# Output product of a gated FFN: where its combined weights lie, which queue carries its side traffic, and how its last visits and its norm are cut

## The chip, the core and the metric

The kernel runs on one core of a Trainium2 chip. A core has TensorE (PE, with its weight loads shown as PEld), VectorE (DVE), ScalarE (ACT), GpSimd (POOL), a queue engine that issues transfers (SP), and sixteen DMA engines that carry out the transfers of all queues. Each engine works through its own list in order; engines wait for each other by semaphores. The metric is the time of one execution on the device in microseconds (us), as the median of several runs.

## What is computed

Two decoder layers on one sequence of 1024 rows and 1024 columns, all in fp32. Layer 0 mixes with differential attention, layer 1 with forgetting attention; after either comes a gated FFN, and after each a LayerNorm of the scaled input plus the result:

```python
D_MODEL, SEQ, DEPTH, D_FF = 1024, 1024, 2, 2816

def conv_ffn(x, w_in, conv_w, conv_b, w_out):
    gate, up = jnp.split(x @ w_in, 2, axis=-1)
    gate = lax.conv_general_dilated(gate, conv_w[:, None, :], ...) + conv_b
    return (jax.nn.silu(gate) * up) @ w_out

for i in range(DEPTH):
    y = diff_attention(h, ...) if i == 0 else forgetting_attention(h, ...)
    h = layer_norm(DEEPNORM_ALPHA * h + y, ln1_g[i], ln1_b[i])
    f = conv_ffn(h, ffn_w_in[i], ffn_conv_w[i], ffn_conv_b[i], ffn_w_out[i])
    h = layer_norm(DEEPNORM_ALPHA * h + f, ln2_g[i], ln2_b[i])
```

## The kernel before

Every fp32 operand is split in a high and a low half (`split`, L83: ScalarE makes the high half at L86, VectorE the low at L88), and a product is three matmuls, high by high, high by low, low by high (`mm3`, L97 to L99). One matmul of 128 rows by 512 columns starts 0.227 us after the last.

**Up product.** `up_steps` makes the FFN's inner values tile by tile, f = 0 to 21, each from seven block products. `take` copies or adds a finished PSUM bank into SBUF (L958 a copy on ScalarE, L960 an addition on VectorE). `gated` does the convolution, the silu and the gating, and stores the tile to DRAM as `ad[f]` (L999). In the last one, f = 21, stands a block of its own (`tile_critical`, L994 to L996) that loads ScalarE's other activation table: ScalarE enters it by a branch.

**Output product.** `down_steps` is a block scheme of seven products m = 1 to 7 over H = 11 k-tiles. With a11, a12, a21, a22 the blocks of the inner values (tiles `ha`, loaded from `ad` by `load_a`) and b11 to b22 those of the weights (`load_b`, from `wd`, into tiles of the pools `pt`, three buffers, and `wst`, two, there named `wb`), it runs four passes over k: m = 1 and 5, then 6 and 3, then 7 and 2, then 4. A pass visits k = 0 to 8 singly and the last two together; the last pass, m = 4, visits 0 to 7 singly and the last `G4` = 3 together. A step is one m and one k: four banks j by three matmuls, 2.72 us. Two combinations of weights are used in more than one pass: T1 = b12 - b11 is made for m = 5 and read again for m = 6, T2 = b22 - T1 is made for m = 6 and read again for m = 4. Before the change both go to DRAM and back, for all eleven k: `sides` stores them (L1078 T1, named `ta`; L1082 T2, `tb`) and `load_b` reloads them into one half of a tile (L1055, L1064) beside a half of `wd`. All combinations are VectorE's, L1071. `make` allots the operand tiles (a ring of six for the left side: `q`, `of` and `p` tiles) and calls `split`.

**Residual, drain and norm.** `load_acc` fetches the eight 128 x 1024 tiles of the scaled residual (`acc` <- `hs`, 512 KB each) into q tiles and one p tile, at step 4 + tt of the product, on SP's queue (L1168). `drain` (L1138, VectorE) adds a finished bank to them. With the last drain of a tile the `Norm` of that tile begins: mean (L1326), squares on ScalarE (L1329, `junk`), root (L1335 to L1343), and `apply`. In `apply` columns from n on are done by VectorE (L1358, L1361), columns below n by ScalarE (L1356) and GpSimd (L1357, L1360), and L1363 stores. For rows tiles 4 to 7 of the last layer n is `PF` = 256.

**What sets the order.** `Ffn.run` walks the steps of the up product and then those of the output product; before step i it calls what is noted for that step (loads, at fixed leads), makes operands until AHEAD = 6 steps ahead, and emits the products. A scheduler then puts the instructions of each engine in one order by their readiness, so that what is emitted late may stand early where an engine is free. GpSimd issues no transfer in this kernel; SP issues all.

## Time and profile before

| | |
|---|---|
| median of 3 runs | 2527.68 us (2524.8 to 2528.6) |
| the profiled execution | 2527.6 us, its span 2525.8 us |
| PE busy | 2460.4 us, 97% of the span |
| DVE busy | 1963.8 us, 78% |
| ACT busy | 1344.6 us, 53% |
| POOL busy | 128.1 us, 5% |
| transfers | 261.67 MB, mean 104 GB/s |

The profile is of one execution. The table above says which engine is the busiest on average; it doesn't say where the time is lost. For that one reads a table of stages (busy time of each engine in stretches of 50 us), then what PE waited for in the stretches where its busy time is short, then the timeline of the engine that it waited for. In a table of stages a row has the stretch, its length, the busy us (and instructions) of PE, PEld, DVE, ACT and POOL, the granted clock as a share of 2.4 GHz, the busy share of the DMA engines and GB/s. In the rows below, `x<-y` means that an instruction writes x from y, a bracket at the end gives the idle time of the engine just before the instruction and what ended it, and a wait reads "engine tile line <- what released it: us in total, times, longest".

In layer 1 the up product ends and the output product begins near 2297 us; it ends with PE at 2512.86. In layer 0 the same runs from about 1028 us on.

### The profile page before, as it was taken

Reading aid. Unit: us, or ns where it says so; the run is one execution under the profiler, and the core shown is the slowest. Engines: PE = TensorE matmul, PEld = TensorE weight load, DVE = VectorE, ACT = ScalarE, POOL = GpSimd, SP = SyncE. Lnnn points to the kernel's source line nnn. Section 1 sums busy time; section 2 is a strip of 40 time slices with the busy share of each in tenths; the row PEclk is TensorE's granted clock in tenths of the full one; section 3 lists DMA queues with packets and bytes.
Section 4 is the critical chain, followed back from the end, with each engine's and each line's share of the span. In section 5 each row is a group of like instructions: output and inputs, shape, how many; then the busy total and the mean of one; then the engine's idle time right before and its main releaser. Section 6 shows DMA issues by size and latency. Waiting matters only on the chain. (4 is left out here: it accounts for less than half of the span.)

```text
span 2525.8 us, 33612 instructions
## 1 busy us (share of the span) xinstructions
PE 2460.4 (97%) x12075; PEld 2021.9 (80%) x12075; DVE 1963.8 (78%) x3770; ACT 1344.6 (53%) x2517; POOL 128.1 (5%) x308
## 2 busy tenths in 40 slices
PE   7999999999999999999999999999999999999997
PEld 5878788787888888788778888888878888888786
DVE  5777777889867667796858888788888667677878
ACT  5666666746544444444546666566465444444444
POOL 0100000001000000000100000000010000000001
PEclk9999999999999999999999999999999999999999
DMA  3111111422322223864411111114222222327744
GB/s 128 34 59 42 43 42 52 167 92 84 109 75 76 100 76 103 315 208 155 158 54 51 51 51 51 46 57 159 91 84 86 98 75 76 100 96 271 246 142 141
DMA packets 94087, 261.67 MB, mean 104 GB/s; under 512 B 11728, under 2 KB 13136, under 8 KB 93920
## 3 DMA queue, kind: packets, MB, share of 16 engines
q1 hardware_dynamic: 93920, 259.53, 30.4%
q8 instruction: 95, 1.56, 0.3%
q14 instruction: 72, 0.59, 0.1%
HBM read 196.44 MB, written 58.85 MB: 101 GB/s over the span
## 5 line engine op out<-in xcount | busy, mean ns | idle before, releaser
L97 PE MATMUL m<-xh,wh 128*128 128x512 f32 x768 | 323.8, 422 | 6.3 <-ACT xh L86 6.2
L99 PE MATMUL m<-xh,wl 128*128 128x512 f32 x768 | 304.9, 397 | 0.0
L98 PE MATMUL m<-xl,wh 128*128 128x512 f32 x768 | 303.9, 396 | 0.2 <-DVE xl L88 0.2
L97 PE MATMUL m<-xh,wo 128*128 128x512 f32 x656 | 255.4, 389 | 2.5 <-ACT pt L958 2.5
L99 PE MATMUL m<-xh,wo 128*128 128x512 f32 x656 | 255.5, 389 | 0.1
L98 PE MATMUL m<-xl,wo 128*128 128x512 f32 x656 | 255.2, 389 | 0.0
L86 ACT ACTIVATE wo<-wg 128x512 fp32r<-128x512 f32 x168 | 106.3, 633 | 226.6 <-PE m L99 218.1
L86 ACT ACTIVATE pt<-m 128x512 fp32r<-128x512 f32 (+1 forms) x240 | 130.0, 553 | 119.7 <-PE m L1225 99.7
L97 PE MATMUL m<-q,wo 128*128 128x512 f32 x472 | 184.1, 390 | 0.0
L98 PE MATMUL m<-q,wo 128*128 128x512 f32 x472 | 183.8, 389 | 0.0
L99 PE MATMUL m<-q,wo 128*128 128x512 f32 x472 | 183.6, 389 | 0.0
L97 PEld LDWEIGHTS m<-xh,wh 128*128 128x128 f32 x768 | 146.7, 191 | 31.0 <-ACT xh L86 6.2
L99 PEld LDWEIGHTS m<-xh,wl 128*128 128x128 f32 x768 | 145.6, 190 | 31.3
L98 PEld LDWEIGHTS m<-xl,wh 128*128 128x128 f32 x768 | 146.7, 191 | 24.9 <-issue 0.8
L86 ACT ACTIVATE wo<-t 128x512 fp32r<-128x512 f32 x132 | 82.8, 627 | 146.6 <-PE m L99 133.3
L88 DVE TENSOR_TENSOR pt<-m,pt 128x512 fp32r<-128x512 f32 (+1 forms) x240 | 149.5, 632 | 9.8 <-ACT pt L86 7.9
L88 DVE TENSOR_TENSOR wo<-wg,wo 128x512 fp32r<-128x512 f32 x168 | 115.3, 687 | 40.2 <-ACT wo L86 39.4
L97 PEld LDWEIGHTS m<-xh,wo 128*128 128x128 f32 x656 | 123.1, 188 | 29.0 <-ACT pt L958 3.3
L99 PEld LDWEIGHTS m<-xh,wo 128*128 128x128 f32 x656 | 123.1, 188 | 26.4 <-DVE wo L88 0.9
L98 PEld LDWEIGHTS m<-xl,wo 128*128 128x128 f32 x656 | 123.1, 188 | 25.5
L410 PE MATMUL s<-q,q 128*128 128x512 f32 (+3 forms) x384 | 135.5, 353 | 3.7 <-ACT q L253 2.5
L403 POOL CAST qz<-q 64x128 fp32r<-64x128 f32 x256 | 88.8, 351 | 952.2 <-PE s L412 670.0
(316 smaller groups left out, 6318.0 us busy)
## 6 DMA issues: line engine op xcount, KB each, us to landing
wst<-in_w SPq DMA_DIRECT2D x48, 512.0 KB, 3.4
t<-in_wi SPq DMA_DIRECT2D x44, 512.0 KB, 4.5
ad<-t SPq DMA_DIRECT2D x44, 512.0 KB, 3.6
ha<-ad SPq DMA_DIRECT2D x88, 256.0 KB, 5.4
wg<-in_wi SPq DMA_DIRECT2D x42, 512.0 KB, 3.3
pt<-in_wd SPq DMA_DIRECT2D x34, 512.0 KB, 3.5
wb<-in_wd SPq DMA_DIRECT2D x42, 256.0 KB, 3.0
wst<-in_wo SPq DMA_DIRECT2D x16, 512.0 KB, 3.5
```

Of the source, the lines that this page charges most:

```text
L86: nc.scalar.activation(hi, src, AF.Copy, scale=1.0 if scale is None else scale)
L88: nc.vector.tensor_tensor(lo, src, hi.bitcast(F32), op=ALU.subtract)
L97: mm(out, wh, xh, start=start, stop=False)
L98: mm(out, wh, xl, start=False, stop=False)
L99: mm(out, wl, xh, start=False, stop=stop)
L403: nc.gpsimd.tensor_copy(qz[r:r + 64, :], q[r:r + 64, qt * P:qt * P + P])
L410: nc.tensor.matmul(sb[:, ks], q[:, qt * P:qt * P + P], kd[:, ks], start=True, stop=False)
```

## The change

Six things are changed. `KH` = 5: T1 and T2 go through DRAM for k = 0 to 4 only, and their stores are issued by GpSimd; for k = 5 to 10 both are kept in halves of three `t` tiles (`hold`), T2 in the place of T1, and only the half of `wd` is loaded. The difference for m = 3 takes turns in the halves of one held `t` tile in place of a new tile each time. The residual is loaded in halves, on GpSimd's queue: the half that is drained first at step 8 + tt, the other at 24 + tt or 40 + tt. While the up product runs, `Ffn.run` makes one operand of the output product ahead before the last step but one and a second before the last, where it made up to six before. The last group of pass 4 is of five k-tiles, `G4` = 5, in both layers. In the last layer's norm of tiles 4 to 7 all columns are VectorE's (`PF` = 0), from `acc` into a `pt` tile and back, and the last tile's final step is two halves with a store each.

```diff
-PF = (256,256,256,256)
+KH = 5
+PF = (0, 0, 0, 0)
-M7, G4 = 15, 3
+M7, G4 = 15, 5
...
+        held = {}
+        def hold(k):
+            if k not in held:
+                t = self.tmp()
+                held[k], held[k + 1] = t[:, lo], t[:, hi]
+            return held[k]
...
             elif n == 1:
-                nc.sync.dma_start(t[:, lo], self.t1[k])
+                if k < KH:
+                    nc.sync.dma_start(t[:, lo], self.t1[k])
                 nc.sync.dma_start(t[:, hi], w[H + k][:, hi])
-                b["t", k], b[22, k] = t[:, lo], t[:, hi]
+                b["t", k], b[22, k] = t[:, lo] if k < KH else hold(k), t[:, hi]
...
             if m == 5:
-                y = sub(b[12, k], b[12, k], b[11, k])
-                nc.sync.dma_start(self.t1[k], y)
+                y = sub(b[12, k] if k < KH else hold(k), b[12, k], b[11, k])
+                if k < KH:
+                    nc.gpsimd.dma_start(self.t1[k], y)
                 return sub(a[21, k], a[21, k], a[22, k], ALU.add), y
             if m == 6:
                 y = sub(b["t", k], b[22, k], b["t", k])
-                nc.sync.dma_start(self.t2[k], y)
+                if k < KH:
+                    nc.gpsimd.dma_start(self.t2[k], y)
...
             if m == 3:
-                x = self.tp.tile([P, 512], F32, tag="t", name=self.nm("ds"))
-                return sub(x, a[12, k], a[21, k]), b[22, k]
+                if k == 0:
+                    held["s"] = self.tmp()
+                return sub(held["s"][:, lo if k % 2 else hi], a[12, k], a[21, k]), b[22, k]
...
-            nc.sync.dma_start(t, self.hs[tt])
             acc.append(t)
             self.acc = acc
+            half(tt, int(tt > 3))
+        def half(tt, c):
+            cs = slice(c * 512, c * 512 + 512)
+            nc.gpsimd.dma_start(acc[tt][:, cs], self.hs[tt][:, cs])
         for tt in range(8):
-            when(4 + tt, load_acc, tt)
+            when(8 + tt, load_acc, tt)
+            when((24 if tt < 4 else 40) + tt, half, tt, int(tt < 4))
...
-            self.make(self.first[i] + (AHEAD if i else 2))
+            n = self.first[i] + (AHEAD if i else 2)
+            if i < self.up:
+                n = min(n, self.first[self.up] + max(0, i + 3 - self.up))
+            self.make(n)
...
-        nc.vector.scalar_tensor_tensor(a[:, h1], a[:, h1], nm, self.g[:, h1], op0=ALU.add, op1=ALU.mult)
+        u = k.tmp(pool=k.tt, tag="pt") if self.final and tt > 3 else a
+        nc.vector.scalar_tensor_tensor(u[:, h1], a[:, h1], nm, self.g[:, h1], op0=ALU.add, op1=ALU.mult)
...
+        parts = (slice(0, 512), slice(512, 1024)) if self.final and tt == 7 else (h1,)
+        for ns in parts:
+            nc.vector.scalar_tensor_tensor(a[:, ns], u[:, ns], y, self.b[:, ns], op0=ALU.mult, op1=ALU.add)
+            if self.final:
+                nc.sync.dma_start(dst[:, ns], a[:, ns])
```

Line numbers move by 1 up to `hold`, by some 10 to 14 in `down_steps` and by 23 to 27 in the norm: L958 is L959 after, L1071 is L1082, L1138 is L1152, L1358 and L1361 are L1383 and L1388. What stands in a row on the engines changes in three places that matter here.

ScalarE, layer 1, where the up product ends and the first operands of the output product are made; `m` is a PSUM bank, `wo` and `oa` are high halves of operands. Before:

```order
L86 ACTIVATE q_21228<-ha_21110 128x512
L86 ACTIVATE oa_21278<-ha_21153 128x512
L86 ACTIVATE wo_21227<-pt_21108 128x512
L958 COPY pt_21245<-m_21212 128x512
L86 ACTIVATE oa_21256<-ha_21112 128x512
L86 ACTIVATE oa_21305<-ha_21155 128x512
```

After:

```order
L87 ACTIVATE q_21261<-ha_21087 128x512
L87 ACTIVATE oa_21311<-ha_21130 128x512
L959 COPY pt_21216<-m_21189 128x512
L87 ACTIVATE wo_21260<-pt_21085 128x512
L87 ACTIVATE oa_21281<-ha_21089 128x512
L87 ACTIVATE oa_21317<-ha_21132 128x512
```

The copy of the bank (L958, now L959) stands one place earlier, ahead of `wo<-pt` in place of behind it.

GpSimd, layer 1, around its branch into the block of the last gate; `acc<-hs` is a half of a residual tile, `ta<-` a store of T1, `tb<-` one of T2. Before, the branch stands between the norm of the layer's attention and the last norm:

```order
L1360 TENSOR_TENSOR acc_16820<-acc_16820,lg_17673 128x256
L1357 TENSOR_TENSOR acc_16822<-acc_16822,lg_17672 128x256
L1360 TENSOR_TENSOR acc_16822<-acc_16822,lg_17673 128x256
L1424 UNCONDITIONAL_BRANCH
L1357 TENSOR_TENSOR acc_21575<-acc_21575,lg_21521 128x256
L1360 TENSOR_TENSOR acc_21575<-acc_21575,lg_21522 128x256
L1357 TENSOR_TENSOR acc_21606<-acc_21606,lg_21521 128x256
```

After:

```order
L1188 DMA acc_21621<-hs 128x512
L1090 DMA ta_117<-wb_21218 128x512
L1188 DMA acc_21646<-hs 128x512
L1188 DMA acc_21668<-hs 128x512
L1188 DMA acc_21692<-hs 128x512
L1090 DMA ta_118<-pt_21252 128x512
L1188 DMA acc_21646<-hs 128x512
L1188 DMA acc_21668<-hs 128x512
L1188 DMA acc_21692<-hs 128x512
L1454 UNCONDITIONAL_BRANCH
L1095 DMA tb_125<-pt_21594 128x512
```

Ahead of the branch stand 19 transfers, of which the last nine are shown; the residual halves of steps 24 and later were pulled ahead of it by the scheduler, those of the p tile come behind it. The same 19 stand there in layer 0.

ScalarE's own branch into that block, with the semaphores that it waits for, DMAHW those of SP's queue and DMASW those of GpSimd's. Before:

```order
L991 ACTIVATE t_21378<-t_21378 128x1024 [waits DVE_49,Activation_49]
L86 ACTIVATE oa_21442<-ha_21298 128x512 [waits DMAHW4_49]
L994 NO_OP [waits DMAHW2_49,DMAHW0_49,DMAHW4_49,Activation_sequencer_49,DMAHW6_49,PE_49,Activation_49]
L1424 UNCONDITIONAL_BRANCH [waits DMAHW2_49,DMAHW1_49,DMAHW3_49,DMAHW0_49,DMAHW4_49,Activation_sequencer_49,DMAHW5_49,DVE_49,DMAHW6_49,PE_49,DMAHW7_49,Activation_49,Pool_49]
L995 ACT_TABLE_LOAD
```

After:

```order
L992 ACTIVATE t_21355<-t_21355 128x1024 [waits DVE_49,Activation_49]
L87 ACTIVATE oa_21419<-ha_21254 128x512 [waits DMAHW7_49]
L995 NO_OP [waits DMAHW2_49,DMAHW0_49,DMAHW4_49,Activation_sequencer_49,DMAHW6_49,PE_49,Activation_49]
L1454 UNCONDITIONAL_BRANCH [waits DMASW6_49,DMASW5_49,DMASW7_49,DMASW4_49,DMAHW0_49,DMASW3_49,DMAHW1_49,DMASW2_49,DMAHW2_49,DMASW1_49,DMAHW3_49,DMASW0_49,DMAHW4_49,Activation_sequencer_49,DMAHW5_49,DVE_49,DMAHW6_49,PE_49,DMAHW7_49,Acti
L996 ACT_TABLE_LOAD
```

The branch now waits for all eight semaphores of GpSimd's queue too.

VectorE, the end of the last layer's norm; `p` is the last tile, `n` are values of one column. Before:

```order
L1358 SCALAR_TENSOR_TENSOR p_21653<-p_21653,nm_23161,lg_21521 128x768
L1339 SCALAR_TENSOR_TENSOR n_4173_23134<-n_4172_23133,n_4171_23132 128x1
L1337 TENSOR_SCALAR n_4176_23162<-n_4176_23162 128x1
L1343 SCALAR_TENSOR_TENSOR n_4172_23133<-n_4173_23134,n_4172_23133 128x1
L1339 SCALAR_TENSOR_TENSOR n_4178_23164<-n_4177_23163,n_4176_23162 128x1
L1355 TENSOR_TENSOR n_4173_23134<-nm_23131,n_4172_23133 128x1
L1361 SCALAR_TENSOR_TENSOR acc_21630<-acc_21630,n_4172_23133,lg_21522 128x768
L1343 SCALAR_TENSOR_TENSOR n_4177_23163<-n_4178_23164,n_4177_23163 128x1
L1355 TENSOR_TENSOR n_4178_23164<-nm_23161,n_4177_23163 128x1
L1361 SCALAR_TENSOR_TENSOR p_21653<-p_21653,n_4177_23163,lg_21522 128x768
```

After:

```order
L1388 SCALAR_TENSOR_TENSOR acc_21668<-pt_23051,n_4154_23041,lg_21493 128x1024
L1366 SCALAR_TENSOR_TENSOR n_4160_23073<-n_4161_23074,n_4160_23073 128x1
L1152 SCALAR_TENSOR_TENSOR p_21712,sums_21491<-p_21712,s_21341 128x512
L1388 SCALAR_TENSOR_TENSOR acc_21692<-pt_23083,n_4160_23073,lg_21493 128x1024
L1349 TENSOR_SCALAR nm_23103<-sums_21491 128x1
L1383 SCALAR_TENSOR_TENSOR pt_23115<-p_21712,nm_23103,lg_21492 128x1024
L1360 TENSOR_SCALAR n_4165_23104<-n_4165_23104 128x1
L1362 SCALAR_TENSOR_TENSOR n_4167_23106<-n_4166_23105,n_4165_23104 128x1
L1366 SCALAR_TENSOR_TENSOR n_4166_23105<-n_4167_23106,n_4166_23105 128x1
L1388 SCALAR_TENSOR_TENSOR p_21712<-pt_23115,n_4166_23105,lg_21493 128x512 x2
```

The passes of 768 columns in place are now of 1024 columns into a `pt` tile and back, the last in two halves; the one-column step for ScalarE's part (L1355) is gone, and the last tile's drain (L1152) stands behind the final pass of the second tile of the four.

## Rows read from the trace of the kernel before

**Rows 1.** Table of stages, 50 us each; busy us (instructions) of each engine.
```profile
1000.00:1050.00 50.00, 48.76 (x215) 40.07 (x214) 41.08 (x64) 26.41 (x43) 0.00 (x0) 1.00 0.71 242
...
2250.00:2300.00 50.00, 48.78 (x215) 40.06 (x214) 40.32 (x59) 25.14 (x39) 0.00 (x0) 1.00 0.57 194
2300.00:2350.00 50.00, 47.91 (x211) 39.33 (x210) 37.72 (x62) 22.58 (x39) 0.00 (x0) 1.00 0.86 305
2350.00:2400.00 50.00, 48.70 (x215) 39.99 (x215) 44.61 (x74) 19.59 (x35) 0.00 (x0) 1.00 0.65 212
```

**Rows 2.** Waits of layer 0, 1000 to 1130 us: total, times, longest.
```profile
PE s L99 <- DVE oa L88: 2.3, 1, 2.3
```

**Rows 3.** Timelines of the end: start, us, instruction, idle before and releaser.
```profile
2492.00 1.28 DVE L1358 SCALAR_TENSOR_TENSOR acc<-acc,nm,lg 128x1024 f32<-128x1024 f32 x1
...
2502.87 0.68 DVE L88 TENSOR_TENSOR wo<-pt,wo 128x512 fp32r<-128x512 f32 x1
...
2512.46 0.40 PE L99 MATMUL s<-wo,oa 128*128 128x512 f32 x1
...
2514.72 1.13 ACT L1329 ACTIVATE junk<-p,nm 128x1024 bf16<-128x1024 f32 x1
...
2520.64 0.33 SPq L1363 DMA_DIRECT2D out<-acc  x1
...
2522.09 0.72 POOL L1360 TENSOR_TENSOR p<-p,lg 128x256 f32<-128x256 f32 x1
```

**Rows 4.** Waits of layer 1, 2250 to 2420 us.
```profile
PE s L99 <- DVE oa L88: 2.1, 1, 2.1
...
PE s L97 <- DVE acc L1138: 1.3, 1, 1.3
PE m L97 <- ACT pt L958: 1.2, 1, 1.2
```

**Rows 5.** Timeline of ScalarE, layer 1, around the end of the up product.
```profile
2284.81 0.63 ACT L86 ACTIVATE oa<-ha 128x512 fp32r<-128x512 f32 x1 [3.08 <-DMA ha<-ad]
...
2285.86 0.57 ACT L958 COPY pt<-m 128x512 f32<-128x512 f32 x1
...
2306.62 1.28 ACT L995 ACT_TABLE_LOAD   x1 [3.65 <-DMA ha<-ad]
```

**Rows 6.** Timeline of VectorE, layer 1, first half of the output product.
```profile
2308.32 0.69 DVE L997 TENSOR_TENSOR t<-t,pt 128x512 f32<-128x512 f32 x1 [4.61 <-ACTq L994]
...
2341.20 0.69 DVE L1071 TENSOR_TENSOR pt<-pt 128x512 f32<-128x512 f32 x1 [0.80 <-DMA pt<-ta]
...
2356.48 0.69 DVE L1071 TENSOR_TENSOR wb<-wb 128x512 f32<-128x512 f32 x1 [1.73 <-DMA wb<-ta]
```

**Rows 7.** Waits of SP's queue, 2250 to 2420 us.
```profile
SPq L1055 <- DMA ta<-pt: 6.9, 3, 2.9
```

**Rows 8.** Transfers issued from 2300 to 2346 us: count, KB, us to landing.
```profile
acc<-hs SPq DMA_DIRECT2D x7, 512.0 KB, 7.3
```

**Rows 9.** Table of stages around the boundary, columns as in rows 1.
```profile
2284.00:2288.00 4.00, 2.78 (x13) 1.96 (x12) 3.19 (x5) 2.75 (x6) 0.00 (x0) 1.00 1.04 400
...
2284.00:2306.60 22.60, 21.38 (x94) 17.36 (x93) 18.90 (x29) 12.04 (x19) 0.00 (x0) 1.00 0.86 300
2306.60:2346.00 39.40, 37.31 (x165) 30.55 (x164) 30.11 (x49) 17.82 (x31) 0.00 (x0) 1.00 0.86 311
```

**Rows 10.** Timeline of TensorE, layer 1: three matmuls.
```profile
2284.88 0.39 PE L99 MATMUL m<-q,wo 128*128 128x512 f32 x1
...
2316.58 0.39 PE L97 MATMUL m<-wo,oa 128*128 128x512 f32 x1
...
2497.80 0.39 PE L97 MATMUL s<-wo,q 128*128 128x512 f32 x1
```

**Rows 11.** Timeline of GpSimd at the end.
```profile
2511.52 1.46 POOL L1357 TENSOR_TENSOR acc<-acc,lg 128x256 f32<-128x256 f32 x1 [635.81 <-ACT acc L1356]
```

**Rows 12.** Transfers issued from 2500 us on.
```profile
out<-p SPq DMA_DIRECT2D x1, 128.0 KB, 1.9
```

More of the change, by code (lines that the diff above doesn't have):

```diff
@@ L1357, in apply @@
             nc.gpsimd.tensor_tensor(a[:, h0], a[:, h0], self.g[:, h0], op=ALU.mult)
-        nc.vector.scalar_tensor_tensor(a[:, h1], a[:, h1], nm, self.g[:, h1], op0=ALU.add, op1=ALU.mult)
+        u = k.tmp(pool=k.tt, tag="pt") if self.final and tt > 3 else a
+        nc.vector.scalar_tensor_tensor(u[:, h1], a[:, h1], nm, self.g[:, h1], op0=ALU.add, op1=ALU.mult)
         if n:
             nc.gpsimd.tensor_tensor(a[:, h0], a[:, h0], self.b[:, h0], op=ALU.add)
-        nc.vector.scalar_tensor_tensor(a[:, h1], a[:, h1], y, self.b[:, h1], op0=ALU.mult, op1=ALU.add)
-        for ns in (h1, h0) if self.final and n else (slice(0, 1024),):
+        parts = (slice(0, 512), slice(512, 1024)) if self.final and tt == 7 else (h1,)
[3 more added lines that the diff above has]
+                nc.sync.dma_start(dst[:, ns], a[:, ns])
+        if not self.final or n:
+            ns = h0 if self.final else slice(0, 1024)
             nc.sync.dma_start(dst[:, ns], a[:, ns])
```

5 lines of the change are left out of this document (3 added, 2 removed).

## The prediction

> **What bounds the kernel now.** I read the table of stages first, fifty us a row. TensorE is busy for 97% of the span, and what the change can win lies in a few places. A row of layer 1 with 48.78, 47.91 or 48.70 us of PE in 50 has lost 1.22, 2.09 and 1.30 us, at the start and in the first half of the output product [rows 1]. Layer 0 loses 1.24 in the row from 1000 [rows 1] and 2.3 in one wait behind it [rows 2]. That is a budget of 8.1 us, plus the tail after the last matmul, which is 12.9 us (2512.86 to 2525.8) [rows 3].
>
> Second, the waits name three stalls in layer 1 [rows 4], of which layer 0 has the first two [rows 1, 2].
> Stall 1 (1.2): the product's PSUM bank waits for the copy of L958. ScalarE runs in order, and the copy stands behind oa<-ha, which had waited 3.08 us for a transfer, and wo<-pt [rows 5].
> Stall 2 (2.1, in layer 0 2.3): TensorE waits for the low half of an operand (oa, L88). The timeline of VectorE shows why: the combination pt<-ta at 2341.20 had to wait for the reload of T1, and the splits that TensorE wants stand behind it [rows 6]. The reload itself went out late: three times, 6.9 us in all, SP waited for stores of T1 before it could issue a reload [rows 7], at a time when each 512 KB of residual, on the same queue, took 7.3 us to land [rows 8].
> Stall 3 (1.3): a drain is late, behind a combination at 2356.48 that waited 1.73 us for another reload of T1 [rows 6].
> Third, the end: the last matmul begins at 2512.46, the last GpSimd step of the norm ends at 2522.81, and 3.0 us later the span ends [rows 3].
>
> **The change, part by part.** The sum is made against the profiled execution, 2527.6 us (span 2525.8 and 1.8 around it), which stands 0.1 below the median of 2527.68.
>
> T1 kept on chip for k of 5 to 10, stores of the others and the residual off SP. Per layer six stores and six reloads of T1 go, and as many of T2: 24 transfers of 256 KB. In the 39.4 us from 2306.6 the trace moves 311 GB/s, 12.3 MB [rows 9]. Of that go seven of the eight residual loads (3.7 MB, now earlier) and seven T1 stores (1.8 MB), which leaves 6.8 MB or 170 GB/s. The reloads of k below 5 stay, but neither their store's landing nor the residual is ahead of them on SP. I take stalls 2 and 3 as gone: 2.3 + 2.1 + 1.3 = 5.7 us. Bounds: 0, if another load takes the place of T1's on VectorE, and 5.7. I take 5.7, since the waits lie in or right behind a stretch that loses nearly half of its bytes.
>
> Stall 1. In the new order of ScalarE the copy stands ahead of wo<-pt, still behind oa<-ha. One ScalarE step moves behind it: half of the 1.05 us between the starts at 2284.81 and 2285.86, 0.52 [rows 5]. Gain 0.5 per layer, 1.0 in all. Bounds: 0, and 2.4 if the oa load lands earlier too. I take 1.0, because the load goes out of SP at the same place.
>
> The residual and stores on GpSimd's queue, ahead of the block boundary. This is the part with a price that the trace lacks: no transfer is issued by GpSimd before. The boundary is the table load of the last gate. ScalarE's branch into it waits for everything issued before it on every queue, and now for 19 transfers of GpSimd as well, 16 of which can't start before the q tiles come free, with the product that reads them, at 2285.1 [rows 10]. The rows: ScalarE gets through at 2306.62 [rows 5]. VectorE's first step after it begins 1.7 us later [rows 6], and in the new order the next operand that TensorE needs is its fifth step of 0.6, done at 2311.4; TensorE wants it at 2316.58 [rows 10]. So 5.2 us are to spare: the boundary may open as late as 2311.8 at no cost. I take layer 0 to have the same, its product being the same. With a cost of c for each issue on GpSimd the sixteenth goes out at 2285.1 + 16c, and lands some 6 us later (an estimate for 256 KB, below the 7.3 of 512 KB [rows 8]). Bounds of c: 0.33, an issue on SP [rows 3], and 1.46, a 128x256 step of GpSimd beside a busy VectorE; the same step takes 0.72 at the end, where VectorE is done [rows 3, 11]. At c = 1.0, my choice, between the two, the last lands at 2307.1: half a us later than now, hidden by the 5.2. At 1.46 it lands at 2314.5 and costs 2.7 us in each layer. The cover is gone at c = 1.29. The bytes give the same picture: 300 GB/s in the 22.6 us before the boundary [rows 9], 6.8 MB, to which 14 halves of 262 KB and one store add 3.9; at the 400 GB/s of a stretch where the DMA engines are full [rows 9] this takes 27 us, and the boundary opens near 2311, just inside. I put the cost at 0 and the bound at 2.7 per layer. Queued behind waiting entries of GpSimd's queue is the store of T1 for k=3 and 4; SP's loads of the next weights into the same buffers wait for those stores, and have some 30 us until TensorE needs them.
>
> Fewer operands ahead, held T1 halves, m=3 in halves of one tile: they change which tile is written, not the count of VectorE or ScalarE steps in front of TensorE. Before the boundary the same operands as now are made. 0, hidden by the spare 5.2 us.
>
> Last group of five instead of three. The last visit to a bank has 15 matmuls of 0.227 us in place of 9, so the drains come 3.4 us apart in place of 2.0. This needs operand k=10 sooner: VectorE finishes its low half at 2503.55 [rows 3]; the group would begin at 2497.8, where k=6 begins now [rows 10], and in the new order of TensorE that half is wanted by the 25th matmul, at 2503.2, 0.3 too soon, as are k=8 and 9 by as much. Cost 0.5 us in layer 1 and, by the same spacing, 0.5 in layer 0. Bounds 0 (if VectorE, which has fewer reloads to wait for, is ahead by then) and 1.0 each.
>
> The norm of the last four tiles on VectorE. Before, 9.95 us pass between the end of TensorE and that of the last GpSimd step, with two 768-wide steps of VectorE, one of ScalarE and two of GpSimd for each of the last tiles. After, for the last tile in order: the drain starts 1.4 late, behind a 1024-wide pass of the second tile; drain 0.6; the third tile's final pass 1.25; the mean 0.25; squares and their readout 1.25 (the squares 1.13 [rows 3]); Ln, Exp and three one-column steps 0.95; two 512-wide halves, each half of a 1.28 step [rows 3], 1.2. Sum 6.9 (the first pass, 1.28 too, lies beside the squares). The last store is 256 KB instead of 128: 0.2 (an estimate for twice the bytes) on the 1.9 that 128 KB take [rows 12]. Before its last bank TensorE waits for the drain of the third, which now stands behind that of the second: some 0.3 longer. Gain 9.95 - 6.9 - 0.2 - 0.3 = 2.5. Bounds 1 (the drain later still) and 4 (order of VectorE without collision).
>
> Sum: -5.7 - 1.0 - 2.5 + 1.0 = -8.2, so 2527.6 - 8.2 = **2519.4**.
>
> **Rivals.** (a) Slower: GpSimd's issues hold up the boundary. One mechanism, at one place, twice. Its price: if an issue is a GpSimd step beside a busy VectorE and an issue as on SP, 1.46 + 0.33 = 1.79, the last lands at 2285.1 + 28.6 + 6 = 2319.7, 7.9 after the spare time is used up; twice that is 15.8, less 8.2: 2535.2. It decides from c = 1.55, where twice the loss equals the gain. For it: VectorE is busy for 18.9 of those 22.6 us [rows 9], and GpSimd's step doubles beside it [rows 3, 11]. Against: an issue moves no data through GpSimd.
> A rule of the Trainium skill speaks for this rival: the page "SBUF — State Buffer", section "SBUF: two separate sides", says that descriptors of GpSimd's transfers are written by GpSimd itself, and that VectorE can lock it out meanwhile. No run here shows such a transfer; the trace agrees so far as GpSimd's doubled step goes. The page "DMA: Bandwidth & Descriptors", section "Anatomy of one DMA — SWDGE (gpsimd) path", gives 2.0 us and the bytes by 436 GB/s for one such transfer; were that 2.6 us the spacing of issues, the estimate would be 2285.1 + 41.6 + 6, 20.9 late, and about 2561; the same section lays most of it on the completion, which would not space the issues.
> (b) About the same: the stalls move. The bytes now crowd the stretch before the boundary (c about 1.46, or slow landings): 2.7 lost per layer, 5.4, so 2519.4 + 5.4 = 2524.8. For it: the thin margin of 0.8 us by bytes. Against: TensorE's operands there are made long before.
> (c) Only the tail is gained, since another load takes the place of T1's in stalls 2 and 3: 2527.6 - 1.0 - 2.5 + 1.0 = 2525.1. The change of hold would then not do what it says. For it: SP still has the loads of ha and of the weights to issue, in the same order; against: the drop in bytes.
>
> **How the numbers follow.** A measurement of this kernel tells about 0.2%, 5.1 us, from no change. The forecast, with its neighbours from 2515.5 (tail 4, stall 1 gone whole, no late operands), or 2514.5 with 1 for the spread of runs, to 2522.5, has 0.54. Rivals (b) and (c) have 0.25 together, all within 0.2%. Rival (a) has 0.21. The range reaches from 2514.5 to 2536, which holds (a) at the price named; about 0.1 lies above and 0.05 below, and some of both is not foreseen. The likeliest case's own range is 2514.5 to 2522.5.
>
> **What would show it.** In the table of stages, the rows from 2300 and 2350 with PE above 49.5. Among the waits, no "PE s L99 <- DVE" of 2 us and no drain of 1.3; the copy's wait near 0.7. GpSimd's issues near 1 us and a table load before 2311.8; a table load after that with TensorE waiting for oa or wo in (5,3) is rival (a) or (b), told apart by the distance of issues on GpSimd. From the last matmul to the end of the span some 10 us in place of 12.9. I am wrong if the reload of T1 still ends a wait of TensorE, or if the table load moves by over 5 us.

## The result, and the profile after

The change made the kernel slower: 2546.44 us (2545.12 to 2548.03) against 2526.92 (2524.8 to 2528.6), four runs each, ratio 1.0081 with the interval 1.0065 to 1.0096. The forecast was 2519.4; the time lies above the range. The profiled execution has a span of 2543.4 us, 17.6 more than before.

The table of stages after, same stretches and columns as [rows 1], with two more of layer 0:

```profile
1000.00:1050.00 50.00, 48.63 (x211) 39.10 (x210) 34.61 (x53) 23.58 (x39) 9.83 (x18) 1.00 0.75 277
1050.00:1100.00 50.00, 43.88 (x182) 34.32 (x180) 41.06 (x68) 19.76 (x36) 3.84 (x7) 0.97 0.69 241
1100.00:1150.00 50.00, 47.77 (x199) 39.29 (x200) 40.29 (x65) 17.95 (x31) 0.00 (x0) 0.93 0.22 70
...
2250.00:2300.00 50.00, 50.00 (x222) 41.27 (x221) 38.01 (x56) 24.57 (x39) 5.84 (x11) 1.00 0.49 165
2300.00:2350.00 50.00, 47.74 (x206) 37.98 (x205) 35.92 (x57) 22.97 (x39) 5.13 (x10) 1.00 0.87 319
2350.00:2400.00 50.00, 41.15 (x170) 32.36 (x169) 41.87 (x70) 15.00 (x26) 3.29 (x6) 0.97 0.43 142
```

The count of matmuls is the better measure here, since at a lower clock each one is longer and TensorE looks busy. A full row has 222 or 223. Layer 1 has 598 in its three rows, before 641 [rows 1]: 43 fewer, at 0.227 us each 9.8 us. Layer 0 has 592, before 647 (215 [rows 1], then 209 and 223): 55 fewer, 12.5 us. So the loss is in the two output products, and 2.9 come back at the end: from the last matmul (2533.00, 0.39 long) to the end of the span pass 10.0 us, before 12.9 [rows 3].

What TensorE waited for after, in layer 0 (1000 to 1130 us), layer 1 (2250 to 2420) and behind it (2420 to 2545), to be held against [rows 2, 4]:

```profile
PE s L98 <- DVE acc L1152: 4.7, 2, 4.0
PE s L99 <- DVE wo L89: 3.7, 3, 2.4
PE m L99 <- DVE wo L89: 0.8, 1, 0.8
...
PE m L98 <- ACT pt L959: 0.2, 1, 0.2
...
PE s L98 <- DVE acc L1152: 3.9, 1, 3.9
PE s L99 <- DVE wo L89: 3.4, 3, 2.2
PE m L99 <- DVE wo L89: 2.1, 2, 1.3
...
PE m L98 <- ACT pt L959: 0.5, 1, 0.5
...
PE s L98 <- DVE acc L1152: 1.2, 1, 1.2
```

The copy (stall 1) fell from 1.2 to 0.5 and 0.2. But where a drain cost 1.3 us, it now costs 3.9 and 4.0, and several waits for low halves (`wo`), 10.0 us in the two layers, are new.

The boundary in layer 1. Where the up product ends, its last matmuls read a q tile; from the last of these to ScalarE's table load passes the time in which the boundary opens. TensorE's timeline of before:

```profile
2297.31 0.39 PE L99 MATMUL m<-q,wo 128*128 128x512 f32 x1
```

After, TensorE's timeline:

```profile
2305.93 0.39 PE L100 MATMUL m<-q,wo 128*128 128x512 f32 x1
```

After, ScalarE's:

```profile
2323.62 1.28 ACT L996 ACT_TABLE_LOAD   x1 [7.08 <-PE m L100]
```

That is 17.7 us after, and 9.3 before (2306.62 [rows 5] less 2297.31): 8.4 later, measured against TensorE's own progress. What filled the DMA engines meanwhile, after: GpSimd's timeline, a row of stages, the transfers issued from 2260 to 2330 us, and VectorE's longer waits.

```profile
2293.51 4.23 POOL L1188 DMA_DIRECT2D acc<-hs  x7 [11.67 <-PE m L100]
...
2304.90 1.92 POOL L1188 DMA_DIRECT2D acc<-hs  x3 [1.30 <-ACT q L87]
2311.69 0.55 POOL L1090 DMA_DIRECT2D ta<-pt  x1 [4.87 <-DVE pt L1082]
```
```profile
2300.00:2320.00 20.00, 19.30 (x84) 15.31 (x83) 12.80 (x19) 6.65 (x10) 4.58 (x9) 1.00 1.03 399
```
```profile
acc<-hs POOLq DMA_DIRECT2D x14, 256.0 KB, 7.5
...
ta<-pt POOLq DMA_DIRECT2D x3, 256.0 KB, 2.3
ta<-wb POOLq DMA_DIRECT2D x2, 256.0 KB, 6.4
```
```profile
2308.01 0.69 DVE L1082 TENSOR_TENSOR ha<-ha,ha 128x512 f32<-128x512 f32 x1 [2.85 <-DMA ha<-ad]
...
2325.26 0.69 DVE L998 TENSOR_TENSOR t<-t,pt 128x512 f32<-128x512 f32 x1 [7.97 <-ACTq L995]
...
2359.56 0.69 DVE L1082 TENSOR_TENSOR pt<-pt 128x512 f32<-128x512 f32 x1 [3.42 <-DMA pt<-in_wd]
2365.38 0.69 DVE L1082 TENSOR_TENSOR wb<-wb 128x512 f32<-128x512 f32 x1 [2.72 <-DMA wb<-in_wd]
```

An issue on GpSimd takes 0.55 to 0.64 us (0.55 for one store, 4.23 / 7, 1.92 / 3). Between its issues GpSimd's list waits too, for the data of T1's stores and for q tiles to come free (1.92, 2.84, 1.30 and 4.87 us). Before, SP sent seven tiles of the residual between 2312.3 and 2336.6, behind the boundary; after, GpSimd sends the same bytes between 2293.5 and 2313.9, ahead of it. From 2300 to 2320 the DMA engines are full (share 1.03, 399 GB/s; in the same 20 us before 0.73 and 242), and VectorE waits 2.85 us for a load of `ha` even ahead of the boundary, then 7.97 at it (before 4.61 [rows 6]). Some 35 us later two reloads end waits of 3.42 and 2.72. SP's own loads pay as well. Six loads of `ha` that SP issued from 2298 to 2308 took a median of 13.1 us to land; six at the same place of the kernel before (2289.4 to 2299.4) took 5.2; and one issued at 2315.1 took 8.4, so that it landed at 2323.5, just ahead of the table load. The last half on GpSimd's queue had landed at 2320.9. After, before, and the load of 2315.1:

```profile
ha<-ad SPq DMA_DIRECT2D x6, 256.0 KB, 13.1
```
```profile
ha<-ad SPq DMA_DIRECT2D x6, 256.0 KB, 5.2
```
```profile
ha<-ad SPq DMA_DIRECT2D x1, 256.0 KB, 8.4
```

Behind the two late reloads comes the drain for which TensorE waits 3.92 us, and then TensorE runs at its lower level for a while (TensorE's timeline, then the stage with its granted clock):

```profile
2380.80 0.80 PE L98 MATMUL s<-wo,oa 128*128 128x512 f32 x1 [3.92 <-DVE acc L1152]
2381.39 0.63 PE L99 MATMUL s<-wo,oa 128*128 128x512 f32 x1
2381.81 0.63 PE L100 MATMUL s<-wo,oa 128*128 128x512 f32 x1
```
```profile
2380.90:2384.10 3.20, 3.20 (x8) 2.55 (x9) 3.20 (x6) 0.28 (x1) 0.00 (x0) 0.50 0.06 21
```

A granted clock of 0.50 is 1.2 GHz in place of 2.4; the matmuls come 0.42 us apart in place of 0.227, eight of them: 1.6 us more.

Before the experiments, a view worked out from the timelines, which they use: the **lead**, from the end of an operand's low half `wo` on VectorE to the first matmul of the step that uses the operand. For the first operand that TensorE needs of those made behind the boundary it was 5.8 us before and is -1.2 after (the matmul, already started on the high half, waited for it). For the 14 steps behind that, the lead before was 6 to 11 us; after, it stays between -2.5 and 1.

### The profile page after: what moved, and what is told of

It reads as the page before. It is cut to its first block, busy times and chain, and to the rows that moved or that the text cites. A ratio compares the mean times of both kernels' runs of the same rounds, so it can differ in the third digit from the quotient of the medians.

```text
span 2543.4 us, 33577 instructions
## 1 busy us (share of the span) xinstructions
PE 2467.9 (97%) x12075; PEld 2022.8 (80%) x12075; DVE 1968.3 (77%) x3767; ACT 1341.2 (53%) x2513; POOL 150.7 (6%) x352
## 5 line engine op out<-in xcount | busy, mean ns | idle before, releaser
L87 ACT ACTIVATE wo<-t 128x512 fp32r<-128x512 f32 x168 | 104.9, 625 | 158.2 <-PE m L100 134.5
L89 DVE TENSOR_TENSOR wo<-t,wo 128x512 fp32r<-128x512 f32 x168 | 115.5, 688 | 46.8 <-ACT wo L87 46.7
```

The source lines that it names most:

```text
L87: nc.scalar.activation(hi, src, AF.Copy, scale=1.0 if scale is None else scale)
L89: nc.vector.tensor_tensor(lo, src, hi.bitcast(F32), op=ALU.subtract)
```

## The experiments

Sixteen kernels were run; ratios are to the kernel before on the same chip, with 95% intervals. They ran on several chips, on which the kernel before took 2522.9 to 2526.9 us, so rows are compared by their ratios. "Drain" is the longest wait of TensorE for L1152 in the two output products; "boundary" is the time from the last matmul on a q tile of the up product to the table load, layer 1.

| kernel | us | ratio | drain, layer 0 / 1 | boundary |
|---|---|---|---|---|
| the change | 2546.4 | 1.0081 [1.0065, 1.0096] | 4.0 / 3.9 | 17.7 |
| res_only: before with the residual's part alone | 2548.2 | 1.0092 [1.0077, 1.0107] | 4.6 / 4.7 | 15.1 |
| gp_whole: whole tiles on GpSimd | 2543.2 | 1.0072 [1.0059, 1.0085] | 4.0 / 4.1 | 17.3 |
| res_late: halves on GpSimd, behind the boundary | 2542.7 | 1.0073 [1.0056, 1.0090] | 3.6 / 4.0 | 10.4 |
| res_pace: halves on GpSimd, paced | 2533.7 | 1.0031 [1.0018, 1.0044] | 3.3 / 3.3 | 10.3 |
| res_tiny: halves on GpSimd, one row each | 2529.8 | 1.0026 [1.0017, 1.0034] | 3.9 / 4.0 | 11.2 |
| res_none: no residual | 2528.2 | 1.0009 [1.0000, 1.0018] | 4.0 / 4.0 | 9.5 |
| half_sp: halves on SP | 2526.2 | 1.0008 [0.9999, 1.0017] | 4.0 / 3.7 | 9.5 |
| res_sp: residual as before | 2520.0 | 0.9985 [0.9976, 0.9994] | 3.4 / 1.9 | 10.0 |
| none_sp1: as before, one row each | 2513.6 | 0.9958 [0.9945, 0.9971] | none | 9.7 |

**The residual's part undone, and alone.**

```diff
# res_sp (from the change; res_only puts the other form into the kernel before)
-            half(tt, int(tt > 3))
...
-            nc.gpsimd.dma_start(acc[tt][:, cs], self.hs[tt][:, cs])
-            when(8 + tt, load_acc, tt)
-            when((24 if tt < 4 else 40) + tt, half, tt, int(tt < 4))
+            nc.sync.dma_start(t, self.hs[tt])
+            when(4 + tt, load_acc, tt)
```

> The changed kernel with one part undone: the residual comes as before, in whole tiles on SP's queue at step 4 + tt. Theory S (the residual, pulled ahead of the block boundary, fills the DMA engines there, the boundary opens 7 us late, VectorE stands still for 8 us and TensorE's lead in operands is gone 30 us later): the table load is back at 11.7 us or so behind the end of the up product's last but one product as in the kernel before, no drain wait of 4 us, about 2521 to 2526 us. Theory H (keeping T1 and T2, and their stores on GpSimd's queue, hold up the reloads of pass 2 whatever the residual does): still 2540 or more, with VectorE waiting for pt<-in_wd by 3 us.

> The kernel before with only the residual moved, in halves on GpSimd's queue at the steps of the change. Theory S: most of the loss comes with this part alone, 2538 to 2548 us. Theory H: within 3 us of the kernel before, 2524 to 2530.

Measured: without the part 0.9985, with it alone 1.0092. The whole loss, and more, is in how the residual is fetched: 0.0096 between the change and res_sp, some 24 us. The other parts together give a gain that just shows, 0.0015 or 3.8 us, where the forecast had 8.2. That 2519.98 us stands beside the forecast of 2519.4 is chance: next to these runs the kernel before took 2523.69, not 2527.6. Theory S expected no drain's wait of 4 us; one of 3.4 is left in layer 0.

**Behind the boundary, and paced.** Two ways to keep the halves on GpSimd but not in one burst ahead of the boundary.

```diff
# res_late: a step of one column on GpSimd, reading the last gate's tile, ahead of each first half
+            nc.gpsimd.tensor_tensor(t[:, 0:1], self.gate_t[:, 0:1], self.gate_t[:, 0:1], op=ALU.mult)
+            nc.gpsimd.tensor_tensor(t[:, 512:513], self.gate_t[:, 0:1], self.gate_t[:, 0:1], op=ALU.mult)
             half(tt, int(tt > 3))
# res_pace: the same ahead of every half, reading the operand made last
+            x = self.made_op[:, 0:1].bitcast(F32)
+            nc.gpsimd.tensor_tensor(acc[tt][:, c * 512:c * 512 + 1], x, x, op=ALU.mult)
             nc.gpsimd.dma_start(acc[tt][:, cs], self.hs[tt][:, cs])
```

> The changed kernel, with a one-column step of GpSimd ahead of each residual half that reads the last gate's tile, so that no residual load can stand ahead of the block boundary; the loads, their queue and their halves stay. Theory S: the boundary opens as in the kernel before and the stalls of 2 to 4 us at the end of pass 1 shrink, about 2520 to 2530 us (a burst of 14 halves now falls behind the boundary, which may cost a few us). Theory H: 2540 or more, as nothing about the reloads is changed.

> The changed kernel; the halves stay on GpSimd's queue, but ahead of each stands a one-column step of GpSimd that reads the operand made last at that step of the product, so that the halves go out one by one, about one in 2.7 us, and none before the boundary. Theory L: with the burst gone the loss goes, 2518 to 2526 us, though the queue is the same. Theory G (a transfer issued by GpSimd is as such what slows SP's loads or the waits behind them): 2535 or more.

In res_late the boundary is nearly back (10.4 us), yet the time hardly moves. This spoke against my first theory, that the boundary's lateness is the cause by itself. The burst now comes behind it: fourteen halves from 2328.18 on (GpSimd's timeline, VectorE's, and the stage):

```profile
2328.18 3.81 POOL L1191 DMA_DIRECT2D acc<-hs  x7
```
```profile
2337.38 0.69 DVE L1083 TENSOR_TENSOR t<-wb 128x512 f32<-128x512 f32 x1 [3.22 <-DMA wb<-in_wd]
2343.21 0.69 DVE L1083 TENSOR_TENSOR ha<-ha,ha 128x512 f32<-128x512 f32 x1 [3.93 <-DMA ha<-ad]
```
```profile
2328.00:2344.00 16.00, 15.43 (x69) 12.44 (x67) 8.25 (x15) 6.94 (x13) 7.83 (x16) 1.00 1.00 370
```

SP's loads of operands share full DMA engines with it, VectorE waits 3.22 and 3.93, and the lead, 4.7 us at the first operand behind the boundary, is below zero some six steps later. What matters is the lead, wherever it is lost. Paced, the lead shrinks slowly, from 5 to below 0 after a dozen steps, and 0.0050 of the 0.0081 go. With 2533.7 us the time lies between the ranges of both theories.

**The queue, or the halves?**

```diff
# half_sp (from the change)
-            nc.gpsimd.dma_start(acc[tt][:, cs], self.hs[tt][:, cs])
+            nc.sync.dma_start(acc[tt][:, cs], self.hs[tt][:, cs])
# gp_whole (from res_sp)
-            nc.sync.dma_start(t, self.hs[tt])
+            nc.gpsimd.dma_start(t, self.hs[tt])
```

> The changed kernel with one word changed: the residual halves are issued by SP in place of GpSimd, at the same steps. Their places in SP's list are then between the loads of operands and weights, from the fourth k-tile on, none ahead of the block boundary. Theory L (the loss is the lead of the operands over TensorE, eaten where 3.7 MB of residual run beside SP's loads in a burst, before the boundary or behind it): the lead stays above 4 us at the step after the boundary and after it, about 2516 to 2523 us. Theory Q (the form of the halves, or their later steps, late for the drains of pass 1): drains wait, 2530 or more.

> The change with one thing undone in part: the residual is fetched in whole tiles of 512 KB at step 4 + tt, as before, but still on GpSimd's queue. It parts the queue from the halves and their steps. Theory (the burst): seven q tiles still come free with one product, and on a queue with nothing else in it seven whole tiles, 3.7 MB, go out at once ahead of the block boundary; the table load of layer 1 then stands 5 us or more later against TensorE's matmuls than with the residual on SP, the operands' lead after it is near zero, and the time is 2541 to 2549, like the change. Rival (the halves, or the order that the scheduler makes with them, are to blame, not the queue): 2518 to 2528, as with the residual on SP in either size (2519.98 and 2526.2).

It is the queue. Seven whole tiles on GpSimd do what fourteen halves did. Its seven issues, 0.54 to 0.65 us each, take under 5 us together; their transfers fill the DMA engines, and the table load waits for a load on SP (gp_whole's timeline of ScalarE):

```profile
2321.32 1.28 ACT L996 ACT_TABLE_LOAD   x1 [5.91 <-DMA ha<-ad]
```

On SP the same halves cost 0.0073 less, 18 us, and whole tiles 0.0087, 22 us. There each waits in line behind the operands' loads that stand ahead of it in the list. The second pair differs in VectorE's order too (see below); in the first the order is nearly the same. half_sp's time lies between the ranges of both theories, and each was half right: the lead stays at 4.5 to 6.6 us over the first eleven steps behind the boundary, as Theory L has it, and drains still wait 4.0 and 3.7, as Theory Q has it.

**Bytes, issues, or order?** Leaving the residual out was meant to give the floor.

```diff
# res_none (from the change; the result lacks the residual)
-            half(tt, int(tt > 3))
+            nc.gpsimd.memset(t, 0.0)
# res_tiny (from the change): zeros by memset, then the halves of one row
-            nc.gpsimd.dma_start(acc[tt][:, cs], self.hs[tt][:, cs])
+            nc.gpsimd.dma_start(acc[tt][:1, cs], self.hs[tt][:1, cs])
# none_sp1 (from res_sp): zeros by memset, then one row on SP
-            nc.sync.dma_start(t, self.hs[tt])
+            nc.sync.dma_start(t[:1], self.hs[tt][:1])
```

> The changed kernel without the residual: its tiles are filled with zeros by GpSimd, nothing of it is loaded, so the result lacks it. Theory L: without these 4.2 MB the lead is never below 5 us in the output product; about 2514 to 2520 us, a floor for what any placing of the residual can reach. Theory H (T1 and T2 held, stores of the others on GpSimd): stalls of 2 to 4 us remain at the end of pass 1, over 2530.

> The change with the bytes of the residual taken away: each half is still issued by GpSimd at the same place, but moves one row of 128 (2 KB in place of 256), the rest of the tile being zeros that GpSimd writes (the result lacks most of the residual). The order of VectorE's steps from the block boundary on is the same as in the change and as without the residual, step for step. Theory (the bytes of the burst cost the loads ahead of it their time): the burst's own cost goes, and the time is that without any residual, 2524 to 2532. Rival (the sixteen issues on a software queue cost it, by GpSimd's descriptors or their locks, or the boundary's wait for that queue): 2540 or more.

> The change without the residual's bytes, but with its eight loads in SP's list at step 4 + tt, each of one row (4 KB in place of 512); the rest of the tile is zeros written by GpSimd. VectorE's order is then nearly that of the variant with the whole residual on SP (2519.98), and not that of the variant without residual (2528.2). Theory (the 8 us between these two are the order that the scheduler makes, T2's combinations close behind the splits that free their tile, with the drain behind them): 2515 to 2522, without a wait of 3 us for a drain in either layer. Rival (the 8 us are something else, for instance the stores on GpSimd or the half clock by itself): 2525 or more, with a drain's wait of 3.5 to 4 us.

Without any residual the kernel takes 2528.2 us (1.0009), more than with all of it on SP (0.9985), and between the ranges of both theories. So there is a second cause. The steps of VectorE from the boundary on, over 200 in each layer, stand in the same order in the change, in res_none, in res_tiny and in res_pace; that settles the bytes: same order, same issues, 254 KB less a half, and 1.0081 falls to 1.0026, some 14 us. TensorE's waits show where these lie. The 10.0 us of waits for low halves `wo` are 0.7 in res_tiny; the waits for drains, 4.7 and 3.9 us in the two layers of the change, are 4.6 and 4.7 without the bytes. So the burst is paid in waits for low halves, between 3 and some 50 us behind the boundary, and the drain's 4 us are not its doing. Pacing takes away nearly as much as dropping the bytes, 0.0050 against 0.0055 (the two intervals overlap). The issues themselves, with their wait at the boundary, are worth some 0.0017 (res_tiny against res_none), 4 us.

none_sp1 moves no more bytes than res_tiny, but its list has eight loads on SP at the old steps, and VectorE's order is nearly that of res_sp. It takes 0.0068 less than res_tiny, 17 us, and 0.0051 less than res_none, 13 us, which has no issues of the residual either. What differs shows on VectorE, from its first step behind the boundary (L998) to the first drains (L1152), with the steps between them left out; first res_tiny, then none_sp1:

```profile
2311.15 0.69 DVE L998 TENSOR_TENSOR t<-t,pt 128x512 f32<-128x512 f32 x1 [5.85 <-ACTq L995]
2333.26 0.68 DVE L1082 TENSOR_TENSOR pt<-pt 128x512 f32<-128x512 f32 x1
...
2344.03 0.69 DVE L1082 TENSOR_TENSOR pt<-pt 128x512 f32<-128x512 f32 x1 [2.87 <-DMA pt<-in_wd]
2349.48 0.69 DVE L1082 TENSOR_TENSOR wb<-wb 128x512 f32<-128x512 f32 x1 [2.35 <-DMA wb<-in_wd]
...
2357.91 1.27 DVE L1152 SCALAR_TENSOR_TENSOR acc<-acc,s 128x512 f32<-128x512 f32 x2
```
```profile
2302.49 0.69 DVE L998 TENSOR_TENSOR t<-t,pt 128x512 f32<-128x512 f32 x1 [4.25 <-ACTq L995]
2328.30 0.68 DVE L1082 TENSOR_TENSOR pt<-pt 128x512 f32<-128x512 f32 x1
...
2337.91 0.68 DVE L1082 TENSOR_TENSOR pt<-pt 128x512 f32<-128x512 f32 x1
2339.79 0.68 DVE L1082 TENSOR_TENSOR wb<-wb 128x512 f32<-128x512 f32 x1
...
2343.41 1.27 DVE L1152 SCALAR_TENSOR_TENSOR acc<-acc,s 128x512 f32<-128x512 f32 x2
```

L1082 here are three of T2's five combinations for the second pass (the second and the fifth, without a wait in both, are left out); each reads a tile that is reloaded into a buffer which a split has just freed. Counted from L998, res_tiny begins them early (22.1 us, none_sp1 25.8), close behind those splits, and two wait 2.87 and 2.35 us for their reload with other splits standing behind them (in the change, with the bytes, 3.42 and 2.72); its first drain comes at 46.8, none_sp1's at 40.9. None_sp1's combinations stand later, so that the reload is done and none of the five waits. In TensorE's waits this is a drain of 4.0 us against none at all:

```profile
PE s L98 <- DVE acc L1152: 4.7, 2, 4.0
PE m L98 <- ACT pt L959: 0.8, 1, 0.8
```

These are res_tiny's two rows of layer 1. None_sp1 has one, for the copy:

```profile
PE m L98 <- ACT pt L959: 0.8, 1, 0.8
```

So where the residual's loads stand in SP's list also decides the order that the scheduler makes of the rest, and that order is worth some 13 us without bytes and issues. No run changes the order and nothing else, so this rests on the pair and on the waits in their traces. The two causes don't add: with all bytes on SP the other order costs 0.0023, some 6 us (half_sp against res_sp, which differ in the halves and their steps too). Why the scheduler places T2's combinations earlier when SP's list lacks these loads was not worked out.

**The other parts.**

```diff
# norm_only: the norm's part alone, put into the kernel before
# no_hold (from res_sp)
-KH = 5
+KH = 11
# g4_3 (from res_sp)
-M7, G4 = 15, 5
+M7, G4 = 15, 3
# ahead6 (from res_sp)
-            if i < self.up:
-                n = min(n, self.first[self.up] + max(0, i + 3 - self.up))
# st_sp (from res_sp)
-                nc.gpsimd.dma_start(self.t1[k], y)
+                nc.sync.dma_start(self.t1[k], y)
...
-                nc.gpsimd.dma_start(self.t2[k], y)
+                nc.sync.dma_start(self.t2[k], y)
```

> The kernel before with only the last layer's norm wholly on VectorE, out of place, the last tile in two halves; the last group stays at three. Both theories: the tail from the last matmul to the end of the span shrinks from 12.9 to about 10 us, 2524 us; the rest of the profile as before.

Measured: 2523.08 us, 0.9999 [0.9990, 1.0009]. In its profile the last matmul begins at 2508.67 and the span ends at 2519.5, so the tail is 10.4 us in place of 12.9. But the last bank's matmul waits longer for the drain ahead of it, 1.62 us in place of 0.79:

```profile
2506.70 0.50 PE L97 MATMUL s<-wo,oa 128*128 128x512 f32 x1 [1.62 <-DVE acc L1138]
```

The stall for `oa` in layer 1 was 3.0 in place of 2.1 in that execution. The tail's gain is there; as a time it can't be told from nothing.

> The changed kernel with the residual as before (whole tiles, SP's queue) and T1 and T2 of all eleven k through DRAM, their stores on GpSimd's queue. It tells what holding T1 and T2 of six k is worth: my prediction put 5.7 us on that and the moved residual together; if holding is what earned res_sp its gain, this is 3 to 6 us slower than res_sp, about 2523 to 2526; if the queue of the stores earned it, it is as fast as res_sp, 2520.

Measured: 2532.22 us, 1.0031 [1.0021, 1.0040]; TensorE waits for drains (4.4 and 4.9) and for `oa` (2.4 and 1.8). Against res_sp the six held tiles are worth 0.0046, 12 us, where 3 to 6 were expected. But VectorE's order differs as well, and no_hold is slower than the kernel before, which sends the same T1 and T2 through DRAM with its stores on SP. How much of the 12 us is the holding, and how much eleven stores a pass on GpSimd's queue, no run parts.

> The change with the residual as before (whole, on SP, step 4 + tt) and the five T1 and T2 stores on SP too, so that GpSimd issues nothing. Theory: with only five stores a pass SP seldom waits for one, and the queue of the stores is worth little: 2518 to 2526, within 0.2% of the 2519.98 with the stores on GpSimd. Rival (a store at the head of SP holds up the loads behind it, as the 6.9 us of SP's waits did before): the waits of SP for stores of T1 come back and the time is 2527 or more.

> The change with the residual as before and without the limit on operands made ahead of the up product's end (up to six again). The prediction put this part at 0. Theory: 2517 to 2523, no difference from 2519.98. Rival (fewer operands ahead leave more of VectorE's and ScalarE's time to the last gate, and the part was worth something): 2526 or more, with the gate's copy late again (a wait of 1 us or more of TensorE for the copy of L959).

> The change with the residual as before and a last group of three k-tiles again. The prediction charged the group of five 0.5 us a layer for operands that come too late and counted 0.3 for later drains. Theory (as predicted): 2518 to 2520, a us or so less than 2519.98, not to be told from it. Rival (five spaces the drains so that VectorE keeps up, and the part is worth more than it costs): 2523 or more, with TensorE waiting for a drain before the last bank and a tail after the last matmul above 10.5 us.

st_sp takes 2517.46 us, 0.9969 [0.9958, 0.9981]: faster than the change and than the kernel before. Its interval overlaps res_sp's, and VectorE's order is another one, so that the queue of the stores as such gains anything is not shown. TensorE's waits in its layer 1 are all short:

```profile
PE m L98 <- DVE p L1152: 0.5, 1, 0.5
PE s L98 <- DVE acc L1152: 0.5, 1, 0.5
PE m L98 <- ACT pt L959: 0.4, 1, 0.4
```

SP's waits for stores of T1, 6.9 us before [rows 7], are down to 0.3 there. ahead6 takes 2522.49, 0.9986 [0.9977, 0.9995], no difference from res_sp, as predicted. g4_3 takes 2524.68, 1.0000 [0.9991, 1.0009], 0.0015 above res_sp with VectorE's order the same up to the end, and above the 2518 to 2520 expected; the intervals overlap, so that five k-tiles are better than three is not shown, but that they cost a us is not borne out either.

**Around the best version.** From st_sp, `LEAD, G = 12, 2` in place of 10 (st_sp_l12), and `when(2 + tt, load_acc, tt)` in place of 4 (st_sp_r2).

> The best version so far (residual whole and both stores on SP, 2517.46) with the loads of the first three passes two steps earlier in what is noted (lead 12 in place of 10). Theory (what is left are waits of 0.5 us, and tiles come free no earlier): 2515 to 2519, no difference. Rival (the order shifts and a drain's wait comes back): 2521 or more.

> The best version so far (2517.46) with the residual, whole and on SP, noted two steps earlier (step 2 + tt), so that its loads stand earlier in SP's list. Theory (on SP a load of the residual waits in line behind the operands' loads, so it can't take their place in a burst): 2515 to 2520. Rival (the bytes come too early also on SP and the lead goes): 2523 or more, with waits of TensorE for the low half wo.

Measured: 2520.58 us, 0.9988 [0.9978, 0.9999], with a wait of 2.0 for a `q` half in each layer, so the longer lead in what is noted is no help; and 2516.69, 0.9980 [0.9969, 0.9990], not to be told from st_sp. The version that stays is st_sp: the change with the residual and the stores of T1 and T2 left on SP.

## Why the prediction was wrong, point by point

**T1 on chip, stalls 2 and 3 gone (5.7).** Half right. SP's waits for stores of T1 are gone in the change, and st_sp has no wait above 0.5 us where the stalls were. But in the change itself the step failed: the stalls did not go but grew, to waits of 3.9 and 4.0 for a drain and up to 2.4 for `wo`. The bound "0, if another load takes the place of T1's" named the way, the reloads from `in_wd`, but it did not reach below zero, and it had to: these reloads are waited for 3.42 and 2.72 us where T1's were waited for 0.80 and 1.73 [rows 6]. Their waits are nearly the same without the residual's bytes (2.87 and 2.35), so they come from VectorE's order and not from full DMA engines. The size of 5.7 is not shown by any run: res_sp and st_sp gain 3.8 and 7.8 us with all parts together.

**Stall 1 (1.0).** Right: 0.7 was expected to remain, 0.5 and 0.2 remained.

**Residual on GpSimd's queue (0, bound 2.7 a layer).** This is the step that failed: a term put at 0 measured some 24 us (the change against res_sp), 14 of them the bytes (res_tiny against the change). It failed in three ways. First, the model by issues: c was chosen as 1.0 and is 0.55 to 0.64, but the sum let the sixteen issues follow each other without a gap, and GpSimd's list also waited 10.9 us between them. The last half left 20.4 us after the first began, as with a c of 1.27, and the boundary opened later still, behind a load of `ha` on SP's own queue. Second, the estimate by bytes, which stood beside it, opened the boundary "near 2311, just inside", with 10.7 MB at 400 GB/s. In the 31.0 us from 2292.6 to 2323.6 the trace after moves 11.4 MB at 368 GB/s. The last matmul on a q tile is 8.6 us later after (2305.93 against 2297.31), so 2311 is 2319.6 on the clock of after; it opened at 2323.62, 4.0 later. I gave the weaker model the word because it had a margin. Third, and dearest: the 5.2 us were called "to spare", as if TensorE's next operand were the only thing that they pay for. (The trace of before has 5.8, since the operand is VectorE's fourth step there and not the fifth.) They are the lead of every operand behind it. By the prediction's own rule the boundary, open 3.2 us past its limit of 2311.8, would have cost 3.2 us a layer; TensorE waited 10.0 us for low halves. res_late shows it too: boundary restored, and still 1.0073, because the same bytes took the lead a little later.

**What the prediction didn't look at.** It followed the change of order at three engines and places, and said that held halves and fewer operands ahead "change which tile is written, not the count". The count is the same; but VectorE's order behind the boundary changed with the residual's loads gone from SP's list, and T2's combinations came to stand where they wait for their reloads. Without bytes this is some 13 us (res_none against none_sp1). A drain's wait of 4 us per layer remains even with no residual at all.

**Fewer operands ahead (0).** Right (ahead6). **Group of five (a loss of 1.0 in all for late operands).** Not borne out: behind 2420 us TensorE waits for no operand in the change, only 1.2 and 0.3 us for drains, and in layer 0 for none behind 1130 us.

**Norm (2.5).** Right: some 10 us were expected from the last matmul to the end, 10.0 were measured, a gain of 2.9, and the drain before the last bank is waited for 0.4 us longer (0.3 expected). As a time norm_only doesn't show it.

**The rivals.** (a) had the sign, but its mechanism, the price of an issue, is refuted by 0.55 to 0.64 us. VectorE was busy for 10.14 of the 12 us from 2288 to 2300, and seven issues in a row took 0.60 each; nothing of a lockout shows here. The rule of the Trainium skill that stood beside it (page "SBUF — State Buffer", section "SBUF: two separate sides": VectorE can lock GpSimd out while it writes descriptors) is stated there for VectorE's steps in a two-port mode; no run here shows whether any step was in one. (b) had the mechanism, crowded bytes, at the price of 5.4; the bytes cost 14. Its argument against, that TensorE's operands "are made long before", is the error in a nutshell: they are made 6 to 11 us before, and a burst of 20 us at 399 GB/s eats that. The mechanism of (c) came about too, at a higher price: the reloads from `in_wd` took the place of T1's. Taken without the residual's part, the sum of the prediction, a gain of 8.2, is not borne out by res_sp (3.8 us, interval 1.5 to 6.1). With the stores on SP too (st_sp) the gain is 7.8 us. That this is near 8.2 is in part luck, for no run shows the single terms at their sizes.

## What to carry to other kernels

A transfer that is moved from a busy queue to an idle one loses the pacing that the busy queue gave it. Ask when its destination comes free, how many come free at once, and what else needs the DMA engines in the time that their bytes take at the full rate. Spare time in front of one operand is the lead of all that follow: it is not free to spend, and its loss is paid later, here in waits for low halves up to some 50 us behind the boundary. And where a scheduler makes the order, compare the whole order of the engine that feeds the bottleneck, also for an edit that only moves transfers.

## What the runs showed of the hardware

Sixteen DMA engines at a share of 1.03 moved 399 GB/s, and then a 256 KB half on GpSimd's queue took 7.5 us from issue to landing (median of fourteen). Of the five 256 KB stores of T1 on the same queue two went out from 2279.7 to 2281.9, with the DMA engines at 0.31, and landed in 2.3; two in the burst took 7.2 and 5.5, and one ahead of both, at a share of 0.71, took 5.7. The two queues share these engines: from 2260 to 2330 us SP's queue took 45.9% of them and GpSimd's 18.7%.

```profile
q1 hardware_dynamic: 4688, 11.34, 45.9%
q0 software_dynamic: 1520, 4.98, 18.7%
```

The Trainium skill says the same (page "DMA: Bandwidth & Descriptors", section "Issuing engines are not separate DMA queues"): transfers from any issuer run on the same engines and interleave, and several issuers save only the time to issue. The trace agrees: beside the burst SP's loads of `ha` took 13.1 us to land in place of 5.2. The prediction had tried the other section of that page, on one GpSimd transfer, as a spacing of issues; its 2.6 us for 256 KB (2.0 and the bytes by 436 GB/s, an estimate) is near the 2.3 of the two stores ahead of the burst and far from the 7.5 in it, and the issues came 0.55 to 0.64 apart where the list didn't wait.

Behind a wait of some 4 us for a drain the granted clock was 0.50, that is 1.2 GHz, for some 3 us in layer 1, and in a stretch from 1100.90 to 1107.60 in layer 0. The kernel before has 1.00 in all of [rows 1]. So a long stall costs more than its own length: in layer 1 3.92 us, and 1.6 more behind it.
